# Five of eight row pairs as seven block products from the third gate-up group, and the first pair's lower parts on GpSimd

## The chip, the cores and the metric

One core of a Trainium2 chip runs the whole layer as one program. The metric is the device time of one execution in microseconds (us), median of several runs. TensorE (PE in the profile) multiplies matrices, VectorE (DVE), ScalarE (ACT) and GpSimd (POOL) work element by element, SyncE (SP) and GpSimd issue the DMA transfers.

## The reference

A layer on 256 tokens of width 2048: a feed-forward network (FFN1), a mixer with a recurrence and windowed attention, and a second FFN. Each FFN is, with weights of 2048 x 11264 and 5632 x 2048 in float32,

```python
def swiglu(x, w_gate_up, w_down):
    gate, up = jnp.split(x @ w_gate_up, 2, axis=-1)
    return (jax.nn.silu(gate) * up) @ w_down

ff = swiglu(rms_norm(x, pre_norm_ffn1[layer]), w_ffn1_gate_up[layer], w_ffn1_down[layer])
x = x + 0.5 * rms_norm(ff, post_norm_ffn1[layer])
```

## The kernel before

**Parts.** Each float32 operand is split into an upper part h, a rounded copy made by ScalarE, and a lower part l = x - h, made by VectorE (`split_act`, L175 to L177). A product of two blocks is three matmuls: h h, l h, h l (`three`). Weights come as tiles `raw` of 128 x 2048 float32 (1 MB), each holding four blocks of 128 x 512: two row blocks by the gate and the up columns. `split_half` makes h and l of 1024 columns at once.

**Groups and pairs.** The gate-up stage of an FFN (`Gated`, `ffn`) runs over 11 groups of 512 gate and 512 up columns, numbered 0 to 10. A group goes over the 2048 rows in eight pairs, 0 to 7, of two row blocks of 128, and accumulates a 2 x 2 grid of PSUM banks c (two token halves by gate and up).

**Plain and seven.** A pair is multiplied plainly, as eight block products (24 matmuls), or in Winograd's form, as seven (21 matmuls). The four pairs of `MIXED_IN`, 2, 4, 5 and 6, are sevens from group 2. A seven needs sums of the left blocks, made once (`sums_of`, four blocks S1 to S4), and sums of the right blocks for each tile: an accumulating DMA issued by GpSimd adds two blocks of the weights onto the tile (`add_second`), two VectorE adds (L985, L986) do the rest. Its order on VectorE is: lower part of the first block, 512 wide and some pairs ahead (`prepare`); then, in `splits`, the lower part of the second half of the tile ("lower"), the two adds, the lower part of the first half ("upper"), that of the changed second half ("last").

**The fold.** Four of the seven products go to banks p of their own. At the end of a group `boundary` folds these into c by eight VectorE adds (L1194 to L1204), each with one input in PSUM, between the products of pairs 6 and 7, and TensorE adds pair 7 to each bank behind its add. Then the parts of the next group's pair 0 are made, then the silu of the gate on ScalarE (L1110) and the product with the up half on VectorE (L1115), four transposes each, and ht, the parts of the down projection's input, with its own sums for some groups (L394 to L398, `MIXED_EARLY`: those of the first eight groups).

**What sets the order.** Everything from group 1 on is under `tc.manual_schedule()`, so each engine takes its instructions in the order in which the code makes them:

```python
for g in range(1, NG):
    first_pairs(g, waiting)
    for u in range(2, last - 1):
        pair_ahead(g, u)
    ...
    boundary(g, gated.splits(g + 1, 0) if g < NG - 1 else splits(0))
```

`pair_ahead(g, u)` makes the parts of pair u + 1 and lets TensorE multiply pair u. The pools hold five h, five l and five `raw` tiles. `plan` and `PREPARED` set the order in which tiles are loaded; a tile's next load is issued on SP once its last part is made (`load_next`). In FFN1's group 1 pair 6 is plain, and its sums are made in that group behind pair 6's parts (`sums_in`).

Of the kernel before, what the change touches and what calls it, by code (L numbers as in the profile page):

```python
# [11 lines left out]
F32 = mybir.dt.float32  # L12
F32R = mybir.dt.float32r
# [4 lines left out]
ALU = mybir.AluOpType  # L18
AX = mybir.AxisListType

P = 128
D = 2048
T = 256
# [25 lines left out]
def hymba_layer_kernel(  # L49
# [19 lines left out]
    nc = tc.nc  # L69
# [4 lines left out]
    hip = ctx.enter_context(tc.tile_pool(name="hip", bufs=5))  # L74
    lop = ctx.enter_context(tc.tile_pool(name="lop", bufs=5))
# [5 lines left out]
    def nm(s):  # L81
        uid[0] += 1
        return f"{s}_{uid[0]}"
# [81 lines left out]
            ls.append(l)  # L165
        return hs, ls

    def split_half(raw, i, hp=hip, lp=lop):
        part = raw[:, i * 1024 : (i + 1) * 1024]
        h = hp.tile([P, 1024], F32R, tag="h", name=nm("h"))  # L170
        l = lp.tile([P, 1024], F32R, tag="l", name=nm("l"))
        split_act(h, l, part)
        return h, l

    def split_act(hi, lo, src):  # L175
        nc.scalar.copy(hi, src)  # L176
        nc.vector.tensor_tensor(lo, src, hi.bitcast(F32), ALU.subtract)  # L177


    def rsqrt_of(ssq, scale, eps):  # L180
# [211 lines left out]
    def sums_of(u, w):  # L392

        nc.vector.tensor_tensor(  # L394
            w[:, S3::2, :], u[:, 0, :].rearrange("p (m t) -> p m t", m=2), u[:, :, P:T], ALU.subtract
        )
        nc.vector.tensor_tensor(w[:, S2, :], w[:, S1, :], u[:, 0, 0:P], ALU.subtract)
        nc.vector.tensor_tensor(w[:, S4, :], u[:, 1, 0:P], w[:, S2, :], ALU.add)  # L398
        return w

    class Blocks:
# [67 lines left out]
        def products(self, u, first, lower, upper, last, order=range(7)):  # L469

            if not self.p:
                self.p = [pa(), pa(), pb(), pb()]
            a, w = self.tiles[u], self.left_sums(u)

            def lhs(k, m):
                return [a[:, k, i, m * P : (m + 1) * P] for i in range(2)]

            def summed(j):
                return [w[:, j, i, :] for i in range(2)]

            def rhs(two, n):
                return [x[:, n * 512 : (n + 1) * 512] for x in two]

            seven = (
                (("p", 0), lhs(0, 0), first),
                (("c", 0, 0), lhs(1, 0), rhs(lower, 1)),
                (("c", 0, 1), summed(S4), rhs(lower, 0)),
                (("p", 1), summed(S1), rhs(upper, 0)),
                (("p", 3), summed(S3), rhs(upper, 1)),
                (("p", 2), summed(S2), rhs(last, 0)),  # L490
                (("c", 1, 0), lhs(1, 1), rhs(last, 1)),
            )
            for i in order:
                at, left, right = seven[i]
                self.three(at, *left, *right)
# [399 lines left out]
    NG = DFF // 512  # L895
# [2 lines left out]

    MIXED_IN = (2, 4, 5, 6)
    PREPARED = {2: -0.5, 4: 0.5, 5: 1.5, 6: 3.5}  # L900
    AWAY = 8
    MIXED = range(0, 20, 2)
    MIXED_EARLY = MIXED[:8]
# [11 lines left out]
    class Gated(Blocks):  # L915
# [23 lines left out]
        def plan(self, opened=False):  # L939

            some = MIXED_IN[1:3] if opened else MIXED_IN[:3]
            self.here = {g: MIXED_IN if g > 1 else some for g in range(1, NG)}
            wanted = []
            for g in range(1, NG):
                for u in range(KT // 2):
                    before = PREPARED[u] if u in self.here[g] else u
                    wanted.append((g * KT // 2 + before, g, u))
            self.wanted = [at[1:] for at in sorted(wanted)]
            self.raws, self.firsts, self.split_of = {}, {}, {}
            self.lasting = []  # L950
            pools = ((rawp, 3), (self.room, 2))
            for pool, n in pools[:: -1 if opened else 1]:
                for _ in range(n):
                    raw = pool.tile([P, 2048], F32, tag="raw", name=nm("raw"), bufs=n)
                    if pool is rawp:
                        self.lasting.append(raw)
                    self.load_next(raw)
# [10 lines left out]
        def prepare(self, g, u):  # L968

            if u not in self.here.get(g, ()):  # L970
                return
            raw = self.raws[g, u]
            h, l = (self.room.tile([P, 512], F32R, tag=t, name=nm(t), bufs=3) for t in ("h1", "l1"))
            split_act(h, l, raw[:, 0:512])
            add_second(raw, self.source(u, g))
            self.firsts[g, u] = h, l

        def splits(self, g, u):

            raw = self.raws[g, u]  # L980
            got = self.split_of[g, u] = []
            if (g, u) in self.firsts:
                b11, b12, b22, b21 = (raw[:, i * 512 : (i + 1) * 512] for i in range(4))
                got.append(split_half(raw, 1))
                nc.vector.tensor_tensor(b22, b11, b22, ALU.add)  # L985
                nc.vector.tensor_tensor(b21, b22, b21, ALU.add)  # L986
                yield
                got.append(split_half(raw, 0))
                yield
                got.append(split_half(raw, 1))  # L990
                self.load_next(raw)
            else:
                got.append(split_half(raw, 0))
                yield
                got.append(split_half(raw, 1))
                self.load_next(raw)
            yield

# [43 lines left out]
    def ffn(gated, w_dn, post_gain, again, gain=None, lead=None, opening=None):  # L1042

        with ExitStack() as st:
# [3 lines left out]
            early = early_cm.__enter__()  # L1048
# [5 lines left out]
            def room_for(tag):  # L1054
                return work.tile([P, 512], F32, tag=tag, name=nm(tag))
# [7 lines left out]
            def sums_again(u):  # L1063

                ht = hts[u].bitcast(F32)
                w = far["pool"].tile([P, 4, P], F32, tag=f"su{u}", name=nm("su"), bufs=1)
                nc.vector.tensor_tensor(
                    w.rearrange("p (k m) t -> p k (m t)", k=2), ht[:, :, 0, :], ht[:, :, 1, :], ALU.add
                )
                a11, a21, a12, a22 = (w[:, i, :] for i in range(4))  # L1070
                nc.vector.tensor_tensor(a22, a21, a22, ALU.subtract)
                nc.vector.tensor_tensor(a21, a11, a21, ALU.subtract)
                nc.vector.tensor_tensor(a11, a22, a11, ALU.subtract)
                nc.vector.tensor_tensor(a12, a12, a11, ALU.add)
                return w

            def even(u):

# [14 lines left out]
            def sums_in(u):  # L1093
                split_act(*sums_begin(u))
# [113 lines left out]
            def first_pairs(g, waiting):  # L1208

                gated.group(g)  # L1210
                some(waiting, 1)
                gated.prepare(g, MIXED_IN[1])
                some(waiting, 1)
                ahead = gated.splits(g, 1)
                some(ahead, 2)
                gated.prepare(g, MIXED_IN[2])
                for one in gated.take(g, 0):
                    one()
                some(waiting, 1)
                ahead = gated.splits(g, 2)  # L1220
                some(ahead, 2)
                some(waiting, 1)
                next(ahead, None)
                for one in gated.take(g, 1):
                    one()

            def pair_ahead(g, u):

                ahead = gated.splits(g, u + 1)
                next(ahead)  # L1230
                if u + 1 == MIXED_IN[1]:
                    gated.prepare(g, MIXED_IN[3])
                next(ahead)
                for one in gated.take(g, u):
                    one()
                for _ in ahead:
                    pass
                if g == 1 and u in sums_at:
                    sums_in(sums_at[u])
                if u == 5 and 1 < g <= AWAY // 2 + 1:  # L1240
                    put_away(2 * g - 4)
                    put_away(2 * g - 3)
# [86 lines left out]
            with tc.manual_schedule():  # L1329
# [3 lines left out]
# [4 lines that stand above are left out]
                    some(gated.splits(g, last), 2)  # L1337
                    if g < NG - 1:
                        gated.prepare(g + 1, MIXED_IN[0])
                    for one in gated.take(g, last - 1):  # L1340
                        one()
                    boundary(g, gated.splits(g + 1, 0) if g < NG - 1 else splits(0))
                    waiting = units(gated.c, rest)
                    some(waiting, 2)
                room_cm.__exit__(None, None, None)
# [290 lines left out]
    with ExitStack() as s2:  # L1636
# [665 lines left out]
        g = gates(1)  # L2302
# [167 lines left out]
```

## Time and profile before

| | |
|---|---|
| median of 3 runs | 1808.65 us (1808.06 to 1808.78) |
| profiled execution | 1808.42 us, its span 1806.6 us |
| TensorE matmuls busy | 1794.5 us, 99% |
| VectorE busy | 1654.2 us, 92% |
| ScalarE busy | 1132.8 us, 63% |
| GpSimd busy | 130.1 us, 7% |

Busy time is the union of an engine's records. Matmuls overlap, so a busy TensorE need not be at its peak. The granted clock of TensorE is 0.999 of 2.4 GHz in the mean. The folds of FFN1's groups 1 and 2 start at 87.27 and 129.10 us, those of groups 6 and 7 at 296.32 and 338.14.

### The profile page before, as it was taken

Reading aid. Unit: us, or ns where it says so; the run is one execution under the profiler, and the core shown is the slowest. Engines: PE = TensorE matmul, PEld = TensorE weight load, DVE = VectorE, ACT = ScalarE, POOL = GpSimd, SP = SyncE. Lnnn points to the kernel's source line nnn. Section 1 sums busy time; section 2 is a strip of 40 time slices with the busy share of each in tenths; the row PEclk is TensorE's granted clock in tenths of the full one; section 3 lists DMA queues with packets and bytes.
Section 4 is the critical chain, followed back from the end, with each engine's and each line's share of the span. In section 5 each row is a group of like instructions: output and inputs, shape, how many; then the busy total and the mean of one; then the engine's idle time right before and its main releaser. Section 6 shows DMA issues by size and latency. Waiting matters only on the chain.

```text
span 1806.6 us, 23864 instructions
## 1 busy us (share of the span) xinstructions
PE 1794.5 (99%) x8368; PEld 1491.4 (83%) x8368; DVE 1654.2 (92%) x2150; ACT 1132.8 (63%) x1487; POOL 130.1 (7%) x158
## 2 busy tenths in 40 slices
PE   9999999999999999999999999999999999999998
PEld 7888888888888888888899888888888888888886
DVE  6999999999999999888888888899999999999997
ACT  7566666655656666566767666556666566566663
POOL 0000000000000101000000000000000000000010
PEclk9999999999999999999999999999999999999999
DMA  9789998888799997954555767889989888699994
GB/s 371 231 256 279 273 277 256 257 259 218 253 324 305 307 285 248 290 158 165 177 169 169 255 198 273 246 238 280 277 270 275 251 248 253 196 318 340 280 315 161
DMA packets 128024, 460.63 MB, mean 255 GB/s; under 512 B 14353, under 2 KB 17169, under 8 KB 126369
## 3 DMA queue, kind: packets, MB, share of 16 engines
q1 hardware_dynamic: 109152, 391.18, 60.9%
q0 software_dynamic: 18608, 67.68, 21.3%
q8 instruction: 65, 1.06, 0.2%
q14 instruction: 55, 0.44, 0.1%
q10 hardware_dynamic: 144, 0.26, 0.0%
HBM read 444.38 MB, written 14.68 MB: 254 GB/s over the span
## 4 chain that ended last, share of the span: by engine, by line
PE 93%; DVE 3%; DMA 2%; ACT 1%; issue 1%; SPq 0%; POOL 0%; DVEq 0%; ACTq 0%; POOLq 0%
PE pa L443 43%; PE pb L443 37%; PE pa L315 6%; PE pa L320 3%; DVE l L177 1%; DMA raw<-in_w_ffn_gate_up_dram 1%; PE pb L1766 1%; DMA X<-in_x_dram 1%; PE pb L1135 1%; PE pa L1135 1%; PE pa L369 0%; PE pa L368 0%; PE pa L367 0%; PE pb L2065 0%; ACT xt L227 0%
## 5 line engine op out<-in xcount | busy, mean ns | idle before, releaser
L176 ACT CAST h<-raw 128x1024 fp32r<-128x1024 f32 (+1 forms) x849 | 831.8, 1009 | 429.9 <-PE pb L443 140.4
L177 DVE TENSOR_TENSOR l<-raw,h 128x1024 fp32r<-128x1024 f32 (+1 forms) x849 | 960.8, 1166 | 75.4 <-ACT h L176 57.0
L443 PE MATMUL pa<-h,xt 128*128 128x512 f32 x1198 | 420.5, 392 | 0.2 <-DVE xt L232 0.2
L443 PE MATMUL pb<-h,xt 128*128 128x512 f32 x1044 | 373.1, 391 | 0.4 <-DVE pb L1197 0.4
L443 PEld LDWEIGHTS pa<-h,xt 128*128 128x128 f32 x1198 | 225.0, 188 | 48.5 <-DVE xt L232 0.6
L443 PEld LDWEIGHTS pb<-h,xt 128*128 128x128 f32 x1044 | 195.9, 188 | 46.9 <-DVE pb L1204 3.8
L443 PE MATMUL pa<-l,xt 128*128 128x512 f32 x599 | 233.6, 390 | 0.0
L443 PE MATMUL pb<-l,xt 128*128 128x512 f32 x522 | 203.3, 390 | 0.0
L443 PE MATMUL pb<-h,ht 128*128 128x512 f32 x428 | 151.2, 389 | 0.0
L443 PE MATMUL pa<-h,ht 128*128 128x512 f32 x428 | 151.1, 389 | 0.0
L443 PEld LDWEIGHTS pa<-l,xt 128*128 128x128 f32 x599 | 112.6, 188 | 22.6 <-DVE l L177 0.7
L148 POOL DMA_DIRECT2D raw<-in_w_ffn_gate_up_dram x77 | 67.3, 874 | 766.2 <-DVE l L177 736.3
L443 PE MATMUL pa<-h,xs 128*128 128x512 f32 x328 | 117.2, 389 | 0.0
L443 PE MATMUL pb<-h,xs 128*128 128x512 f32 x328 | 114.3, 389 | 0.0
L443 PEld LDWEIGHTS pb<-l,xt 128*128 128x128 f32 x522 | 98.0, 188 | 18.9
L315 PE MATMUL pa<-xt,h 128*128 128x512 f32 x448 | 109.9, 393 | 0.0
L315 PEld LDWEIGHTS pa<-xt,h 128*128 128x128 f32 x448 | 81.5, 188 | 15.3
L443 PEld LDWEIGHTS pb<-h,ht 128*128 128x128 f32 x428 | 80.4, 188 | 16.6
L443 PEld LDWEIGHTS pa<-h,ht 128*128 128x128 f32 x428 | 80.3, 188 | 16.6
L443 PE MATMUL pa<-l,ht 128*128 128x512 f32 x214 | 83.3, 389 | 0.0
L443 PE MATMUL pb<-l,ht 128*128 128x512 f32 x214 | 83.3, 389 | 0.0
L443 PEld LDWEIGHTS pa<-h,xs 128*128 128x128 f32 x328 | 61.6, 188 | 12.7
(340 smaller groups left out, 2531.7 us busy)
## 6 DMA issues: line engine op xcount, KB each, us to landing
raw<-in_w_ffn_gate_up_dram SPq DMA_DIRECT2D x350, 512.0 KB, 6.3
raw<-in_w_ffn_down_dram SPq DMA_DIRECT2D x176, 512.0 KB, 8.3
raw<-in_w_mix_in_dram SPq DMA_DIRECT2D x94, 512.0 KB, 4.8
raw<-in_w_ffn_gate_up_dram POOLq DMA_DIRECT2D x77, 512.0 KB, 8.3
raw<-in_w_ffn_down_dram POOLq DMA_DIRECT2D x42, 512.0 KB, 8.7
ht<-away SPq DMA_DIRECT2D x24, 512.0 KB, 10.5
raw<-in_w_mix_out_dram SPq DMA_DIRECT2D x24, 512.0 KB, 5.5
away<-ht SPq DMA_DIRECT2D x16, 512.0 KB, 7.4
```

The costliest lines, as they stand in the source:

```text
L148: nc.gpsimd.dma_start(raw[:, 0:1024], src[:, 512:1536], accum_op=ALU.add)
L176: nc.scalar.copy(hi, src)
L177: nc.vector.tensor_tensor(lo, src, hi.bitcast(F32), ALU.subtract)
L315: nc.tensor.matmul(slot[f], weights(hs, kk, f), xcol(xt, k), start=(k == 0), stop=(k == KT - 1))
L320: nc.tensor.matmul(slot[f][:, 0:T], weights(ls, kk, f), xcol(xt, kh * 8 + kk, 0), start=False, stop=False,)
L443: nc.tensor.matmul(self.bank(at), lhs, rhs, start=(n == 1), stop=n in (ends, self.of[at]), skip_group_check=n > ends,)
L1135: nc.tensor.transpose(bank[:, o : o + P], zs[m][:, k * P : (k + 1) * P], ident)
L1766: nc.tensor.matmul(dst, left[a], right[b], start=first and i == 0, stop=last and i == 2)
```

## The change

From group 3 (`FIVE_FROM`) pair 3 is a seven too, so that the sevens are 2 to 6. The sums of pair 3's left blocks are made in group 2 (`sums_apart`) and put into places of the x tiles that sevens don't read. The first block of pair 5 gets a buffer of its own (`spare`), and the loading order follows `PREPARED_FIVE`. The lower parts of pair 0 of groups 2 to 10 are subtracted on GpSimd (`by=nc.gpsimd`).

```diff
-    def split_half(raw, i, hp=hip, lp=lop):
+    def split_half(raw, i, hp=hip, lp=lop, by=nc.vector):
...
-    def split_act(hi, lo, src):
+    def split_act(hi, lo, src, by=nc.vector):
         nc.scalar.copy(hi, src)
-        nc.vector.tensor_tensor(lo, src, hi.bitcast(F32), ALU.subtract)
+        by.tensor_tensor(lo, src, hi.bitcast(F32), ALU.subtract)
...
     MIXED_IN = (2, 4, 5, 6)
     PREPARED = {2: -0.5, 4: 0.5, 5: 1.5, 6: 3.5}
+    ADDED = 3
+    FIVE = (2, 3, 4, 5, 6)
+    PREPARED_FIVE = {2: -0.5, 3: 0.5, 4: 1.5, 5: 2.5, 6: 3.5}
+    FIVE_FROM = 3
...
-            self.here = {g: MIXED_IN if g > 1 else some for g in range(1, NG)}
+            self.here = {
+                g: FIVE if g >= FIVE_FROM else MIXED_IN if g > 1 else some for g in range(1, NG)
+            }
...
+            if g >= FIVE_FROM and u == FIVE[3]:
+                h, l = self.spare(g)
...
-                got.append(split_half(raw, 0))
+                got.append(split_half(raw, 0, by=by))
                 yield
-                got.append(split_half(raw, 1))
+                got.append(split_half(raw, 1, by=by))
                 self.load_next(raw)
...
+            def sums_apart(u):
+                x = gated.tiles[u].bitcast(F32)
+                whole = room_for("z").rearrange("p (k t) -> p k t", k=2)
+                nc.vector.tensor_tensor(whole, x[:, :, 0, :], x[:, :, 1, :], ALU.add)
+                ws = sums_of(whole, room_for("s").rearrange("p (j t) -> p j t", j=4))
+                gated.sums[u] = [
+                    [gated.tiles[v][:, 0, i, P:T] for i in range(2)] for v in MIXED_IN
+                ]
+                for j, (hi, lo) in enumerate(gated.sums[u]):
+                    split_act(hi, lo, ws[:, j, :])
...
+                if u == 2 and g >= FIVE_FROM:
+                    gated.prepare(g, FIVE[3])
...
+                if u == 5 and g == FIVE_FROM - 1:
+                    sums_apart(ADDED)
...
-                    boundary(g, gated.splits(g + 1, 0) if g < NG - 1 else splits(0))
+                    boundary(g, gated.splits(g + 1, 0, nc.gpsimd) if g < NG - 1 else splits(0))
```

Over the program TensorE has 48 matmuls of 512 columns fewer, VectorE 44 instructions more, ScalarE 40, and GpSimd 52: 36 subtractions of 128 x 1024 and 16 DMA issues.

On VectorE, behind the fold that closes group 5 of FFN1, there stood before (`l_...` of 1024 columns from `raw_486` are pair 0's lower parts, the 512-wide one is the first block of pair 4, `raw_489` is pair 1):

```order
L1204 TENSOR_TENSOR pb_1982<-pb_1982,s_2285 128x512
L177 TENSOR_TENSOR l_2320<-raw_486,h_2319 128x1024
L177 TENSOR_TENSOR l_2324<-raw_486,h_2323 128x1024
L1115 SCALAR_TENSOR_TENSOR z_2329<-pa_1980,scales,z_2329 128x512
L177 TENSOR_TENSOR l_419_2339<-raw_492,h_418_2338 128x512
L1115 SCALAR_TENSOR_TENSOR s_2331<-pb_1982,scales,s_2331 128x512
L177 TENSOR_TENSOR l_2345<-raw_489,h_2344 128x1024
```

and there stands now, at the same place (the 512-wide one is the first block of pair 3):

```order
L1237 TENSOR_TENSOR pb_2009<-pb_2009,s_2318 128x512
L1148 SCALAR_TENSOR_TENSOR z_2362<-pa_2007,scales,z_2362 128x512
L177 TENSOR_TENSOR l_428_2372<-raw_486,h_427_2371 128x512
L1148 SCALAR_TENSOR_TENSOR s_2364<-pb_2009,scales,s_2364 128x512
L177 TENSOR_TENSOR l_2378<-raw_489,h_2377 128x1024
```

Pair 0's two subtractions are gone from between the fold and the gate products; they are on GpSimd. On VectorE in the same group pair 3 was, between the last part of pair 2 (`raw_483`) and the first of pair 4 (`raw_492`):

```order
L177 TENSOR_TENSOR l_2415<-raw_483,h_2414 128x1024
L177 TENSOR_TENSOR l_2445<-raw_486,h_2444 128x1024
L177 TENSOR_TENSOR l_2449<-raw_486,h_2448 128x1024
L177 TENSOR_TENSOR l_2480<-raw_492,h_2479 128x1024
L985 TENSOR_TENSOR raw_492<-raw_492 128x512
```

and is now (`h_240_1402` is the spare buffer, for the first block of pair 5):

```order
L177 TENSOR_TENSOR l_2448<-raw_483,h_2447 128x1024
L177 TENSOR_TENSOR l_2478<-raw_486,h_2477 128x1024
L997 TENSOR_TENSOR raw_486<-raw_486 128x512
L998 TENSOR_TENSOR raw_486<-raw_486 128x512
L177 TENSOR_TENSOR h_240_1402<-raw_495,h_240_1402 128x512
L177 TENSOR_TENSOR l_2487<-raw_486,h_2486 128x1024
L177 TENSOR_TENSOR l_2516<-raw_486,h_2515 128x1024
L177 TENSOR_TENSOR l_2522<-raw_492,h_2521 128x1024
```

Two instructions of pair 3 became five, and the first block of pair 5 moved in among them. On VectorE in FFN1's group 2 the new sums stand between the last part of pair 6 (`raw_489`) and pair 7's parts (`raw_483`), ahead of the next group's first block and the fold:

```order
L177 TENSOR_TENSOR l_1177<-raw_489,h_1176 128x1024
L1102 TENSOR_TENSOR z_1182<-xt_124 128x512
L394 TENSOR_TENSOR s_1184<-z_1182 128x2x128
L397 TENSOR_TENSOR s_1184<-s_1184,z_1182 128x128
L398 TENSOR_TENSOR s_1184<-z_1182,s_1184 128x128
L177 TENSOR_TENSOR xt_124<-s_1184,xt_124 128x128
L177 TENSOR_TENSOR xt_125<-s_1184,xt_125 128x128 x3
L177 TENSOR_TENSOR l_1201<-raw_483,h_1200 128x1024
```

Eight instructions are new there; ScalarE has four casts of 128 x 128 at the same place.

## Rows read from the trace of the kernel before

**Rows 1.** Stretches: us, busy us (instructions) by engine, granted clock, DMA share, GB/s.

```profile
129.10:170.90 41.80, 41.80 (x190) 34.46 (x189) 39.82 (x48) 26.18 (x31) 3.49 (x4) 1.00 0.93 277
379.90:421.70 41.80, 41.80 (x190) 34.48 (x189) 38.98 (x45) 25.45 (x30) 3.51 (x4) 1.00 0.88 253
492.83:600.00 107.17, 107.17 (x473) 88.54 (x473) 103.92 (x128) 70.02 (x88) 10.53 (x12) 1.00 0.96 301
```

**Rows 2.** Chain that ended last, in order of time: start, us, what.

```profile
357.29 2.72 PE pa L443 x12
```

**Rows 3.** Waits of TensorE's weight loads: us in total, times, longest.

```profile
PEld pb L443 <- DVE pb L1204: 3.8, 18, 0.2
```

**Rows 4.** Timeline of VectorE from one fold on: start, us, instruction [idle before].

```profile
296.32 0.69 DVE L1194 TENSOR_TENSOR pa<-pa,z 128x512 f32<-128x512 f32 x1
...
301.90 2.35 DVE L177 TENSOR_TENSOR l<-raw,h 128x1024 fp32r<-128x1024 f32 x2
304.16 0.74 DVE L1115 SCALAR_TENSOR_TENSOR z<-pa,scales,z 128x512 f32<-128x512 f32 x1
304.82 0.68 DVE L177 TENSOR_TENSOR l<-raw,h 128x512 fp32r<-128x512 f32 x1
305.42 0.75 DVE L1115 SCALAR_TENSOR_TENSOR s<-pb,scales,s 128x512 f32<-128x512 f32 x1
306.09 4.09 DVE L177 TENSOR_TENSOR l<-raw,h 128x1024 fp32r<-128x1024 f32 x4
...
312.68 0.69 DVE L177 TENSOR_TENSOR ht<-z,ht 128x512 fp32r<-128x512 f32 x1
...
314.88 3.48 DVE L177 TENSOR_TENSOR l<-raw,h 128x1024 fp32r<-128x1024 f32 x3
318.64 1.22 DVE L177 TENSOR_TENSOR l<-raw,h 128x1024 fp32r<-128x1024 f32 x1 [0.28 <-ACT h L176]
319.90 0.69 DVE L985 TENSOR_TENSOR raw<-raw 128x512 f32<-128x512 f32 x1
...
321.23 4.12 DVE L177 TENSOR_TENSOR l<-raw,h 128x512 fp32r<-128x512 f32 x4
```

**Rows 5.** Timeline of VectorE ahead of that fold, pairs 5 and 6.

```profile
287.07 2.59 DVE L177 TENSOR_TENSOR l<-raw,h 128x1024 fp32r<-128x1024 f32 x2 [0.81 <-ACT h L176]
...
291.03 5.38 DVE L177 TENSOR_TENSOR l<-raw,h 128x1024 fp32r<-128x1024 f32 x5
```

**Rows 6.** Timeline of ScalarE around that fold.

```profile
287.34 1.06 ACT L176 CAST h<-raw 128x1024 fp32r<-128x1024 f32 x1 [0.31 <-PE pb L443]
...
302.67 4.93 ACT L176 CAST h<-raw 128x512 fp32r<-128x512 f32 x6
```

**Rows 7.** Timeline of TensorE in that fold: the last matmul of bank c[0][1].

```profile
301.90 0.40 PE L443 MATMUL pa<-h,xt 128*128 128x512 f32 x1
```

**Rows 8.** Timeline of VectorE in FFN1's group 1, sums of pair 6.

```profile
80.96 0.68 DVE L1084 TENSOR_TENSOR z<-xt 128x512 f32<-128x512 f32 x1
...
84.39 2.96 DVE L177 TENSOR_TENSOR l<-raw,h 128x1024 fp32r<-128x1024 f32 x3 [0.26 <-ACT h L176]
```

**Rows 9.** Timeline of TensorE in the fold behind them.

```profile
90.14 0.50 PE L443 MATMUL pb<-h,xt 128*128 128x512 f32 x1 [0.40 <-DVE pb L1197]
```

**Rows 10.** Timelines of GpSimd (a fold; the end) and of VectorE (the end).

```profile
296.76 0.88 POOL L148 DMA_DIRECT2D raw<-in_w_ffn_gate_up_dram  x1 [15.42 <-DVE l L177]
...
1800.65 1.26 POOL L769 TENSOR_TENSOR X<-X,y 128x512 f32<-128x512 f32 x1 [0.83 <-ACT y L768]
...
1800.53 1.53 DVE L784 SCALAR_TENSOR_TENSOR X<-pb,r,X 128x512 f32<-128x512 f32 x3
```

**Rows 11.** Accumulating DMA issues: all of gate-up; single ones. KB, us to landing.

```profile
raw<-in_w_ffn_gate_up_dram POOLq DMA_DIRECT2D x77, 512.0 KB, 8.3
...
raw<-in_w_ffn_gate_up_dram POOLq DMA_DIRECT2D x1, 512.0 KB, 6.8
raw<-in_w_ffn_gate_up_dram POOLq DMA_DIRECT2D x1, 512.0 KB, 9.9
```

More of the change, by code (lines that the diff above doesn't have):

```diff
@@ L171, in split_half @@
         l = lp.tile([P, 1024], F32R, tag="l", name=nm("l"))
-        split_act(h, l, part)
+        split_act(h, l, part, by)
         return h, l
-    def split_act(hi, lo, src):
+    def split_act(hi, lo, src, by=nc.vector):
         nc.scalar.copy(hi, src)
-        nc.vector.tensor_tensor(lo, src, hi.bitcast(F32), ALU.subtract)
+        by.tensor_tensor(lo, src, hi.bitcast(F32), ALU.subtract)
     def rsqrt_of(ssq, scale, eps):
@@ L478, in summed @@
             def summed(j):
-                return [w[:, j, i, :] for i in range(2)]
+                return w[j] if isinstance(w, list) else [w[:, j, i, :] for i in range(2)]
             def rhs(two, n):
@@ L945, in plan @@
                 for u in range(KT // 2):
-                    before = PREPARED[u] if u in self.here[g] else u
+                    at = PREPARED_FIVE if g >= FIVE_FROM else PREPARED
+                    before = at[u] if u in self.here[g] else u
                     wanted.append((g * KT // 2 + before, g, u))
@@ L972, in prepare @@
             raw = self.raws[g, u]
-            h, l = (self.room.tile([P, 512], F32R, tag=t, name=nm(t), bufs=3) for t in ("h1", "l1"))
+            if g >= FIVE_FROM and u == FIVE[3]:
+                h, l = self.spare(g)
+            else:
+                h, l = (
+                    self.room.tile([P, 512], F32R, tag=t, name=nm(t), bufs=3) for t in ("h1", "l1")
+                )
             split_act(h, l, raw[:, 0:512])
@@ L976, in prepare, with splits @@
             self.firsts[g, u] = h, l
-        def splits(self, g, u):
+        def splits(self, g, u, by=nc.vector):
             raw = self.raws[g, u]
@@ L1075, in sums_again, with spare @@
                 return w
+            spared = {}
+            def spare(g):
+                pool = early if g < AWAY - 1 else late
+                if pool not in spared:
+                    spared[pool] = pool.tile([P, 2, 512], F32R, tag="ht", name=nm("h1"))
+                return [spared[pool][:, i, :] for i in range(2)]
+            gated.spare = spare
+            def sums_apart(u):
[8 more added lines that the diff above has]
+                    split_act(hi, lo, ws[:, j, :])
             def even(u):
@@ L1211, in first_pairs @@
                 some(waiting, 1)
-                gated.prepare(g, MIXED_IN[1])
+                sevens = FIVE if g >= FIVE_FROM else MIXED_IN
+                gated.prepare(g, sevens[1])
                 some(waiting, 1)
@@ L1215, in first_pairs @@
                 some(ahead, 2)
-                gated.prepare(g, MIXED_IN[2])
+                gated.prepare(g, sevens[2])
                 for one in gated.take(g, 0):
```

## The prediction

> **What bounds the kernel now.** I read three views in turn: the stretches by group, the waits of TensorE's weight loads, and VectorE's timeline through one gate-up group. In a middle group of FFN1 TensorE is busy for the whole 41.80 us and VectorE for 39.82, or 38.98 in a group without the small sums for the down projection; the granted clock is 1.00 [rows 1]. TensorE starts a matmul of 512 columns every 2.72/12 = 0.2267 us [rows 2]. So TensorE is the bound, but only just: at 18 of the 20 group boundaries it already waits up to 0.2 us for VectorE's last fold add, L1204 [rows 3]. The reader should see there that the fold at a boundary has no slack: what reaches it later is lost.
>
> VectorE's 39.82 us is not its whole need, since records overlap and dependent ones leave gaps, so I count from start to start. I call the start of L1194 in a fold T. From [rows 4]: the fold's eight adds take 301.90 - 296.32 = 5.58; pair 0's two 1024-wide lower parts 304.16 - 301.90 = 2.26, or 1.13 each; the two gate products 0.66 and 0.67, with a 512-wide lower part of 0.60 between; ht and sums 314.88 - 312.68 = 2.20. In a seven the first lower part with its following add takes 319.90 - 318.64 = 1.26 and the two adds 321.23 - 319.90 = 1.33. A seven therefore needs 0.60 + 1.26 + 1.33 + 2 x 1.13 = 5.45, a plain pair 2.26. A group before: 4 x 5.45 + 4 x 2.26 + 5.58 + 1.33 + 2.20 = 39.95 of 41.82; the other 1.87 is waiting. Most of that waiting is for ScalarE's upper part (0.28 in [rows 4], 0.81 in [rows 5], more in starts that leave no idle record), and ScalarE in turn waits for TensorE to release one of five buffers [rows 6]. So VectorE cannot run further ahead than those buffers let it. It meets the fold just in time in every group.
>
> **What TensorE saves.** A pair as seven products takes 21 matmuls for 24. Eight groups in each of two FFNs: 16 x 3 x 0.2267 = 10.9 us, 0.68 per group. A group would be 41.82 - 0.68 = 41.14.
>
> **What VectorE gets.** From group 3 pair 3 costs 5.45 for 2.26, and pair 0's 2.26 leaves for GpSimd: 5 x 5.45 + 2 x 2.26 + 9.11 = 40.88. That would fit below 41.14 if nothing waited; but four waits remain or appear, and each follows from the order of the instructions.
> - In pairs 5 and 6 the last part needs ScalarE's cast, which starts after the second add. [Rows 5] show five subtractions at 291.03 in 5.38, where 4 x 1.13 + 0.68 = 5.20; I take 0.14 for each: 0.28.
> - Pair 0's two subtractions stood between the fold and the first gate product, and covered the time in which TensorE finishes the bank that the product reads. That bank's last matmul ends at 301.90 + 0.40 = 302.30, T + 5.98 [rows 7]; with 0.07 for the signal the product starts at T + 6.05, not T + 5.58: 0.47 lost.
> - The next, 512-wide, subtraction needs a cast that ScalarE starts at 302.67, behind the two gate activations [rows 6]; at about 0.6 for it, a little over half of the 1.06 that 1024 takes there, that is T + 6.95, when VectorE is free at 6.05 + 0.66 = 6.71: 0.24.
> - 0.13 for two casts that come a little late (ht, pair 4's lower part): my estimate.
>
> Sum 40.88 + 1.12 = 42.00: VectorE, not TensorE, sets the group, and it is 0.18 longer than before. Bounds: waits of nothing give 41.14 (TensorE's), all of the former 1.87 give 42.75. Added up in order, such a cycle reaches T + 8.2 with the gate products, 10.5 with pair 1, 11.1 with the first block of pair 4, 18.2 with pair 2, ht and sums, 23.6 with pair 3 (first block of pair 5 at 21.4), 29.1 with pair 4 (first block of 6 at 26.8), 34.1 with pair 5, 39.1 with pair 6, and the next fold at 42.0. TensorE starts pair 2 at T + 19.0 and one seven every 4.76 after it, so the parts are ready for it, and of the buffers none holds VectorE: only the fold is late. Groups 3 to 8 carry the small sums, 9 and 10 do not: their 2.20 - 2 x 0.60 = 1.0 leaves 41.0, below 41.14, and the whole 0.68 is won. Per FFN: 6 x 0.18 - 2 x 0.68 = -0.3.
>
> **The new sums for pair 3.** They are made once per FFN, in group 2, behind the last part of pair 6 and ahead of pair 7's parts, with four casts on ScalarE ahead of pair 7's first cast. Behind them stand pair 7, the next group's first block and the fold. The trace has nearly this in group 1: the same three sums and one 512-wide split, at the same place. They take 84.39 - 80.96 = 3.43 until pair 7's subtraction starts [rows 8], and TensorE then stood idle 0.40 in the fold [rows 9]. It lost so little because in group 1 pair 6 is plain, which costs VectorE 5.45 - 2.26 = 3.2 less and TensorE 0.68 more. In group 2 pair 6 is a seven, and VectorE comes to this place pinned by the buffers of [rows 5, 6], so what it saved early in the group on pair 0 is no lead. The cost is 3.43 at least; four narrow casts for one wide make it at most 3 x 0.6 more, 5.2. A quarter of the width is nearer to the lower end: 3.8. Hidden wholly, as most of it was in group 1, it would be 0.
>
> **GpSimd's part.** Its 512-wide add of two SBUF tensors took 1.265 beside VectorE's L784, which reads PSUM, and those three kept their usual 1.53 together [rows 10]. 1024 wide I take twice that at most, 2.53. It starts behind the DMA issue that ends at 296.76 + 0.88 = 297.64, T + 1.3 [rows 10]; two end by T + 6.4. The fold's adds, each with one input in PSUM, fill that time, and VectorE's next subtraction stands at T + 6.95; TensorE reads pair 0 from T + 7.2 (six matmuls behind the bank of [rows 7]). So I cost it at nothing. If it ended later, each further us would hold up pair 0.
>
> **DMAs.** 16 more accumulating loads of 512 KB. A group then moves 277 x 41.8 + 524 KB, near 12.1 MB in 42.0 us: 288 GB/s. The down stage had 301 with TensorE never idle [rows 1]. In time it is closer: behind their issue, the loads of pairs 5 and 6 have about 8.6 and 8.2 us before the adds that read them (first block done at T + 21.4 and 26.8, issue 0.4 later, adds at 30.4 and 35.4). The median landing is 8.3, one of pair 6, the last of its group, took 6.8, a slow one 9.9 [rows 11]. I take no wait, since these two stand in the quieter part of the group, as that of 6.8 did; 9.9 - 8.2 = 1.7 is the bound.
>
> **The sum.** Per FFN 3.8 - 0.3 = 3.5; twice, 7.0. The profiled execution took 1808.42 (span 1806.6 and 1.8 around it), 0.23 under the median of 1808.65. 1808.42 + 7.0 = 1815.4. Its own range: sums at 3.4 to 5.2 and the cycle 0.2 either way, so 1812 to 1821.
>
> **Rivals.**
> - Faster: VectorE is not the bound. If its waits come to 0.26 or less per group for my 1.12 and the sums are hidden as in group 1, the 10.9 is kept: 1797.5. For it speaks that idle time of 1.87 stands there today; against it that the ledger leaves 0.26. Chance 0.12.
> - The sums are hidden, the rest as forecast: 1808.42 - 0.6 = 1807.8. Against it: group 2's seven at pair 6. 0.08.
> - The sums cost, but groups stay TensorE's: 1808.42 + 7.6 - 10.9 = 1805.1. 0.07.
> - The accumulating loads come late, 0.5 to 1.7 in each of 12 to 16 groups, say 1 in 14: 1815.4 + 14 = 1829. The landing times allow it. 0.13.
> - GpSimd blocks VectorE. If a subtraction of VectorE could not start or run while GpSimd's is under way, 36 x 2.53 = 91 would be added at worst, 1906; it decides once GpSimd ends later than T + 6.95. Against it: [rows 10], and 0.5 us of room. 0.03. The Trainium skill (SBUF — State Buffer, "SBUF: two separate sides") states such a lock: GpSimd and a VectorE instruction with two SBUF inputs exclude each other for a whole instruction. By that rule the fold, with one input in PSUM, runs beside GpSimd, and the trace agrees as far as L784 shows; no row has the other pairing.
>
> **The numbers.** The forecast has 0.57. What this kernel's measurement can tell is about 0.2%, 3.6 us: slower is the forecast, the late loads and the lock, 0.73; same the two middle rivals, 0.15; faster 0.12. A range of 1804.5 to 1825 holds the forecast, the middle rivals and half of the late loads, some 0.8.
>
> **What would show it.** Folds 42.0 apart in groups 3 to 8 and 41.1 in 9 and 10; TensorE waiting some 0.9 per fold for L1230 and L1234; 45.6 between the folds of groups 1 and 2, TensorE idle about 3.8 at the second; GpSimd's two subtractions inside the fold at 2.3 to 2.5 each; VectorE waiting before the first gate product. I am wrong if folds lie 41.1 apart throughout, or if VectorE stands waiting for the accumulating loads before L997, or if fold adds beside GpSimd's subtractions run longer than 0.7.

## The result and the profile after

The changed kernel takes 1826.36 us (median of 4 runs, 1825.73 to 1827.27) against 1808.57 (4 runs, 1808.06 to 1808.78): 1.0100 times as long, 95% interval 1.0087 to 1.0112. The forecast was 1815.4, with a range to 1825.0. The sign was right, the size was not: slower by 17.8 us, not 7. The profiled execution took 1825.73 us, its span 1824.0 (before 1806.6), at a granted clock of 0.999.

From the page of the changed kernel: busy time by engine, and the chain that ended last, by engine.

```profile
PE 1794.1 (98%) x8320; PEld 1480.8 (81%) x8320; DVE 1668.3 (91%) x2194; ACT 1149.3 (63%) x1527; POOL 228.4 (13%) x210
PE 72%; DVE 14%; DMA 7%; issue 4%; ACT 2%; SPq 0%; DVEq 0%; POOL 0%; ACTq 0%
```

TensorE has 48 matmuls fewer, yet its union of records is as long as before (1794.5): the shares of busy time say nothing of the loss. The chain does: before, 93% of it was TensorE; now 21% of it is VectorE and DMA.

In the lines after, the fold is L1227 to L1237 (before L1194 to L1204), the gate products L1148, the two adds of a seven L997 and L998. From the starts of L1227 in VectorE's timeline come the distances between one fold and the next, in us; "group 2" ends with the fold that closes group 2.

| | 2 | 3 | 4 | 5 | 6 | 7 | 8 | 9 | 10 |
|---|---|---|---|---|---|---|---|---|---|
| FFN1 before | 41.83 | 41.80 | 41.81 | 41.80 | 41.81 | 41.82 | 41.81 | 41.79 | 41.20 |
| FFN1 after | 45.22 | 42.46 | 42.03 | 43.16 | 42.46 | 42.67 | 43.11 | 42.09 | 41.49 |
| FFN2 before | 41.83 | 41.80 | 41.82 | 41.79 | 41.81 | 42.06 | 41.79 | 41.81 | 41.19 |
| FFN2 after | 45.21 | 42.96 | 42.94 | 43.14 | 42.05 | 42.91 | 42.65 | 42.08 | 41.46 |

Summed over both FFNs, after less before: group 2 +6.8; groups 3 to 8 +10.6, of which 12 x 0.22 = 2.6 is the undisturbed distance of 42.03 and 8.0 lies above it; groups 9 and 10 +1.1. That is 18.5; the rest of the program gave 1.1 back, which makes the span's 17.4.

The waits of the changed kernel, us in total, times, longest (before, TensorE waited 3.8 us for the last fold add [rows 3]):

```profile
PEld pa L443 <- DVE pa L1227: 16.9, 16, 2.7
PEld pb L443 <- DVE pb L1230: 16.4, 20, 0.9
DVE raw L997 <- DMA raw<-in_w_ffn_gate_up_dram: 7.5, 10, 1.1
DVE z L1148 <- PE pa L443: 6.4, 18, 0.4
```

TensorE waits at every fold for VectorE, as forecast, though in 16 of the 20 at the first add already and not only from L1230 on. New, and in the forecast only as a rival and a sign of being wrong, is that VectorE stands ten times at the first add of a seven. VectorE's timeline through FFN1's group 5 shows where (start, us, instruction [idle before]; it answers to [rows 4, 5]):

```profile
217.18 0.69 DVE L1227 TENSOR_TENSOR pa<-pa,z 128x512 f32<-128x512 f32 x1
...
223.20 0.75 DVE L1148 SCALAR_TENSOR_TENSOR z<-pa,scales,z 128x512 f32<-128x512 f32 x1 [0.35 <-PE pa L443]
224.17 0.69 DVE L177 TENSOR_TENSOR l<-raw,h 128x512 fp32r<-128x512 f32 x1 [0.22 <-ACT h L176]
...
253.70 0.69 DVE L997 TENSOR_TENSOR raw<-raw 128x512 f32<-128x512 f32 x1 [0.68 <-DMA raw<-in_w_ffn_gate_up_dram]
254.43 0.69 DVE L998 TENSOR_TENSOR raw<-raw 128x512 f32<-128x512 f32 x1
255.04 5.38 DVE L177 TENSOR_TENSOR l<-raw,h 128x1024 fp32r<-128x1024 f32 x5
260.34 0.69 DVE L1227 TENSOR_TENSOR pa<-pa,z 128x512 f32<-128x512 f32 x1
```

With T = 217.18 the gate product starts at T + 6.02 and the block at T + 6.99 (forecast 6.05 and 6.95). At T + 36.5 the adds of pair 6 wait 0.68 for their accumulating load, and behind them only the last two parts of pair 6, pair 7 and one block are left before the fold, so that the fold is late by what they wait. All ten waits stand at this place, pair 6's first add, each in another group from 3 to 8. In eight of these groups the distance lies above 42.03 by that wait, within 0.03; in the other two (FFN1's group 5 and FFN2's group 8) 0.4 more lies elsewhere. GpSimd's timeline of the same group:

```profile
217.62 0.86 POOL L148 DMA_DIRECT2D raw<-in_w_ffn_gate_up_dram  x1 [14.30 <-DVE l L177]
218.19 5.08 POOL L177 TENSOR_TENSOR l<-raw,h 128x1024 fp32r<-128x1024 f32 x2
...
245.10 0.86 POOL L148 DMA_DIRECT2D raw<-in_w_ffn_gate_up_dram  x1 [4.73 <-DVE l L177]
```

The two subtractions run from T + 1.01 to T + 6.09, beside the fold and the wait behind it. The load for pair 6 is issued at 245.10 and would have been read at 253.70 - 0.68 = 253.02, 7.9 us on; the median landing of these loads is now 8.6 us (8.3 before [rows 11]).

In groups 9 and 10 no add waits for a load, and still the fold is later than before. VectorE's and ScalarE's timelines in FFN1's group 9:

```profile
388.58 0.69 DVE L1227 TENSOR_TENSOR pa<-pa,z 128x512 f32<-128x512 f32 x1
...
406.19 1.23 DVE L177 TENSOR_TENSOR l<-raw,h 128x1024 fp32r<-128x1024 f32 x1 [0.35 <-ACT h L176]
...
410.95 2.59 DVE L177 TENSOR_TENSOR l<-raw,h 128x1024 fp32r<-128x1024 f32 x2 [0.34 <-ACT h L176]
...
430.67 0.69 DVE L1227 TENSOR_TENSOR pa<-pa,z 128x512 f32<-128x512 f32 x1
```

```profile
409.87 1.05 ACT L176 CAST h<-raw 128x1024 fp32r<-128x1024 f32 x1 [0.98 <-PE pa L443]
```

At T + 22.4 VectorE, at pair 3's last part, waits for a cast, which waits for TensorE to release a buffer. From there to the next fold it works without a pause: 430.67 - 410.95 = 19.7 us. 22.4 + 19.7 is the 42.09 of the table, whatever spare time VectorE had earlier in the group.

### The profile page after: what moved, and what is told of

Its sections match the earlier page's. It is cut to its first block, busy times and chain, and to the rows that moved or that the text cites. A ratio compares the mean times of both kernels' runs of the same rounds, so it can differ in the third digit from the quotient of the medians.

```text
span 1824.0 us, 23998 instructions
## 1 busy us (share of the span) xinstructions
PE 1794.1 (98%) x8320; PEld 1480.8 (81%) x8320; DVE 1668.3 (91%) x2194; ACT 1149.3 (63%) x1527; POOL 228.4 (13%) x210
## 4 chain that ended last, share of the span: by engine, by line
PE 72%; DVE 14%; DMA 7%; issue 4%; ACT 2%; SPq 0%; DVEq 0%; POOL 0%; ACTq 0%
PE pa L443 31%; PE pb L443 28%; DVE l L177 7%; PE pa L315 6%; DMA raw<-in_w_ffn_gate_up_dram 6%; PE pa L320 3%; ACT h L176 2%; DVE raw L997 1%; DVE raw L998 1%; PE pa L369 1%; PE pa L368 1%; PE pa L367 1%; DVE pb L1230 1%; DVE z L1229 1%; PE pb L1804 1%
## 5 line engine op out<-in xcount | busy, mean ns | idle before, releaser
L176 ACT CAST h<-raw 128x1024 fp32r<-128x1024 f32 (+1 forms) x881 | 850.1, 1002 | 399.1 <-DVE raw L1346 85.6
L177 DVE TENSOR_TENSOR l<-raw,h 128x1024 fp32r<-128x1024 f32 (+1 forms) x829 | 936.1, 1166 | 64.9 <-ACT h L176 47.3
L443 PE MATMUL pb<-h,xt 128*128 128x512 f32 x1012 | 363.4, 394 | 7.9 <-DVE pb L1230 7.8
L443 PEld LDWEIGHTS pb<-h,xt 128*128 128x128 f32 x1012 | 190.1, 188 | 59.4 <-DVE pb L1230 16.4
L443 PE MATMUL pa<-l,xt 128*128 128x512 f32 x583 | 228.0, 391 | 0.0
L443 PE MATMUL pb<-l,xt 128*128 128x512 f32 x506 | 197.5, 390 | 0.0
L148 POOL DMA_DIRECT2D raw<-in_w_ffn_gate_up_dram x93 | 81.0, 871 | 687.3 <-DVE l L177 498.8
L177 POOL TENSOR_TENSOR l<-raw,h 128x1024 fp32r<-128x1024 f32 x36 | 91.3, 2722 | 0.0
L148 POOL DMA_DIRECT2D raw<-in_w_ffn_down_dram x42 | 36.4, 866 | 378.6 <-DVE la L177 328.6
```

The source lines that it names most:

```text
L148: nc.gpsimd.dma_start(raw[:, 0:1024], src[:, 512:1536], accum_op=ALU.add)
L177: by.tensor_tensor(lo, src, hi.bitcast(F32), ALU.subtract)
L443: nc.tensor.matmul(self.bank(at), lhs, rhs, start=(n == 1), stop=n in (ends, self.of[at]), skip_group_check=n > ends,)
```

## The experiments

Each is an edit of the changed kernel; folds are counted as in the table. "Before" ran beside them at 1808.85 (the new sums left out, and both repairs), at 1808.75 (GpSimd's part alone, the sevens alone, the sums earlier, the loads earlier) and at 1808.91 (the other four).

### GpSimd's part alone

No group has a fifth seven; GpSimd keeps pair 0.

```diff
-    FIVE_FROM = 3
+    FIVE_FROM = 99
```

> Four sevens as before, no new sums, pair 0's lower parts of groups 2 to 10 on GpSimd. Theory (GpSimd runs beside the fold at no cost, VectorE has 1.87 us of waiting per group that takes up the new wait of 0.35 to 0.47 before the first gate product): folds 41.8 us apart, 1808 to 1809.5. Rival (the new waits behind the fold, 0.57 per group, or a block of VectorE by GpSimd, are lost in full): 18 x 0.57 = 10 us or more, 1819 and up.

1808.33 us (10 runs), ratio 0.9998 (0.9989 to 1.0008). Folds 41.79 to 41.82 apart, 41.2 in group 10. The wait for the gate product is there (18 times, 6.9 us) and costs nothing, since VectorE waits later in the group anyway. So beside four sevens GpSimd's part is free, and what the change loses comes with the fifth.

### The sevens alone

Pair 0's lower parts go back to VectorE.

```diff
-  boundary(g, gated.splits(g + 1, 0, nc.gpsimd) if g < NG - 1 else splits(0))
+  boundary(g, gated.splits(g + 1, 0) if g < NG - 1 else splits(0))
```

> The changed kernel with pair 0's lower parts left on VectorE. Theory (VectorE sets the group): each group from 3 on gets 2.26 us of work more and loses the waits of 0.35 and 0.22 behind the fold, 1.7 x 16 = 27 us, 1850 to 1856. Rival (GpSimd's subtractions hold VectorE up about as much as they take from it): 1820 to 1832.

1843.77 us, ratio 1.0194 (1.0179 to 1.021): below the band expected, and far above the rival's. The undisturbed distance in groups 3 to 8 is 43.50, 1.47 more than with GpSimd. The ledger gives 2.26 less the 0.47 and 0.24 that pair 0 covers again, 1.55. Waits of 0.2 to 1.3 for loads stand in eight of those groups, and no wait for casts is left. Groups 3 to 8 add 14.6 us to the changed kernel's, groups 9 and 10 2.5, of which 0.8 is a wait for a load in FFN2's group 9: in those the two waits for casts (0.35 and 0.34 in the changed kernel's group 9) are gone, so that a part of the added work fills them.

### The new sums left out

Pair 3 takes the sums of pair 2, so the output is not the layer's.

```diff
                 if u == 5 and g == FIVE_FROM - 1:
-                    sums_apart(ADDED)
+                    gated.sums[ADDED] = gated.sums[MIXED_IN[0]]
```

> The changed kernel without the new sums: pair 3 is multiplied with the sums of pair 2, so its output is not the layer's, and the eight VectorE instructions and four ScalarE casts of group 2 are left out. If the sums cost what the distance of the folds of groups 1 and 2 says, the fold that closes group 2 comes 41.8 us behind the one before (45.2 with the sums), everything behind stays as it is in the changed kernel, and the time is 1826.4 - 2 x 3.4 = 1819.6. Rival: the delay in group 2 gave later groups a lead in their loads, which is lost without it; then the waits for the accumulating loads of pair 6 grow and the time stays above 1822.

1820.28 us, ratio 1.0063 (1.0048 to 1.0078): 6.1 less than the changed kernel. Group 2 takes 41.82 and 41.81. Groups 9 and 10 stay within 0.02; groups 3 to 8, with nine waits for loads, take 1.1 more together, single ones from 0.9 less to 1.1 more. The sums cost 3.4 per FFN at their place.

### The sums earlier in group 2

```diff
-                if u == 5 and g == FIVE_FROM - 1:
+                if u == 2 and g == FIVE_FROM - 1:
                     sums_apart(ADDED)
```

> The changed kernel with pair 3's sums made in group 2 behind pair 3's parts, not behind pair 6's. Theory (the sums cost 3.4 us per FFN because nothing but the fold follows them; earlier, VectorE's waiting for buffers takes them up): folds of groups 1 and 2 some 41.8 to 42.3 apart instead of 45.2, 1819 to 1820.5. Rival (VectorE has no time for them anywhere in group 2): 1825 to 1827.

1821.67 us, ratio 1.0072 (1.0057 to 1.0087). Group 2 takes 43.17 and 43.16 where 41.8 to 42.3 was expected: of 3.4 only 2.0 came back. The run without the sums shows what can take them up. VectorE's timeline in its group 2 (FFN1, T = 87.36):

```profile
107.64 1.23 DVE L177 TENSOR_TENSOR l<-raw,h 128x1024 fp32r<-128x1024 f32 x1 [0.83 <-ACT h L176]
109.68 1.22 DVE L177 TENSOR_TENSOR l<-raw,h 128x1024 fp32r<-128x1024 f32 x1 [0.81 <-ACT h L176]
...
119.92 2.59 DVE L177 TENSOR_TENSOR l<-raw,h 128x1024 fp32r<-128x1024 f32 x2 [0.81 <-ACT h L176]
```

At T + 20.3, 22.3 and 32.6 VectorE waits for casts, which wait for TensorE to release a buffer. Work ahead of such a wait can fill it. Behind the sums' place in the changed kernel stands none of the three, behind the new place two. The run with both repairs (below) has the sums behind ht, ahead of all three, and group 2 takes 42.29 and 42.27. The same eight instructions cost 3.4, 1.35 or 0.47 by how many of these waits stand behind them. (Behind ht the load of pair 6 came late besides in three of eight cases, by 0.46 to 0.96, in FFN2 of other runs below.)

### The loads of pairs 5 and 6 earlier

Their first blocks, behind which the loads are issued, are made earlier: that of pair 5 behind ht, that of pair 6 one pair sooner.

```diff
                 some(waiting, 1)
+                if g >= FIVE_FROM:
+                    gated.prepare(g, FIVE[3])
                 next(ahead, None)
...
-                if u == 2 and g >= FIVE_FROM:
-                    gated.prepare(g, FIVE[3])
-                if u + 1 == MIXED_IN[1]:
+                if u + 1 == (3 if g >= FIVE_FROM else MIXED_IN[1]):
                     gated.prepare(g, MIXED_IN[3])
```

> The changed kernel with the first blocks of pairs 5 and 6, and so their accumulating loads, some 4 and 5 us earlier from group 3. Theory (in groups 3 to 8 the folds are 42.4 to 43.2 apart for 42.0 because these loads have 8 us and take longer): VectorE's waits for DMA at the first add go from 7.5 us to under 1, folds near 42.1, 1817 to 1820. Rival (16 more loads fill the DMA engines): the waits stay, 1824 to 1828.

1822.74 us, ratio 1.0078 (1.0063 to 1.0093): 3.6 less, half of what was expected. No add waits for a load any more, yet groups 3 to 8 give back only 2.9 of the 8 that they had too much; 1.7 more come from groups 9 and 10, and the rest of the program lost 1.4 in the profiled execution. Of groups 3 to 8 five lie at 42.17 to 42.23 (0.14 over 42.03, since one cast in pair 5 lost the subtraction that covered it); seven have 42.3 to 42.9, with waits between T + 4 and T + 12, most of them for casts. Ordinary loads play a part in these: by the order of its casts, ScalarE's waits for them in groups 3 to 8 come to 16.8 us in this run and to at most 4.6 in the changed kernel (its other 29.5 us there are for accumulating loads). So one wait was in part exchanged for another.

The more telling rows are in group 9. VectorE's timeline there:

```profile
388.26 0.69 DVE L1227 TENSOR_TENSOR pa<-pa,z 128x512 f32<-128x512 f32 x1
...
409.73 3.50 DVE L177 TENSOR_TENSOR l<-raw,h 128x1024 fp32r<-128x1024 f32 x3 [0.26 <-ACT h L176]
```

Its work per group is the same, but the block of pair 6 (0.60) now stands ahead of the last wait, which is at pair 3's upper part, one instruction earlier than in the changed kernel. From pair 3's last part to the fold VectorE now works for 19.0 us (an estimate, with 1.13 for the upper part) instead of 19.7. Groups 9 and 10 fall to 41.64 and 41.05 (42.09 and 41.49 in the changed kernel). What sets their length is when the buffer comes and the work behind it, not the sum of the work.

### Five sevens in groups 9 and 10 alone

Groups without small sums and without late loads; the new sums are made in group 8, behind ht.

```diff
-    FIVE_FROM = 3
+    FIVE_FROM = 9
...
+                if g == FIVE_FROM - 1:
+                    sums_apart(ADDED)
...
-                if u == 5 and g == FIVE_FROM - 1:
-                    sums_apart(ADDED)
```

> Five sevens in groups 9 and 10 alone, the sums in group 8 behind ht; all else as before, with GpSimd's part. Theory (from the last buffer that TensorE releases VectorE has 19.7 us of work to the fold while TensorE needs less, so the fold is late though the group's sum of work is small): folds 8 to 9 and 9 to 10 at 42.1 and 41.5 apart, for 41.8 and 41.2, 1809 to 1811. Rival (what counts is the sum of VectorE's work, 41.0): 41.14 and 40.5, 1805 to 1807.

1811.33 us (10 runs), ratio 1.0014 (1.0004 to 1.0023). The folds that close groups 9 and 10 come after 42.06 and 41.48 in FFN1 (42.75, with a wait of 0.46 for TensorE within the fold before and one of 0.34 for a cast at T + 33.7, and 41.49 in FFN2). Group 8, with the sums, takes 42.25 and 43.19, the latter with a late load of 0.96. Of the 41.1 that my ledger gives for them nothing is to be seen, though in FFN1 nothing but their own work and the release is left to delay them.

### A block ahead of the gate products

The sums behind ht, the early loads, and the first block of pair 3 between the fold and the gate products, to fill the 0.47 in which VectorE waits there.

```diff
-                gated.prepare(g, sevens[1])
+                if g < FIVE_FROM:
+                    gated.prepare(g, sevens[1])
...
                     boundary(g, gated.splits(g + 1, 0, nc.gpsimd) if g < NG - 1 else splits(0))
+                    if FIVE_FROM <= g + 1 < NG:
+                        gated.prepare(g + 1, FIVE[1])
```

> The changed kernel with the early loads of e3, pair 3's sums still earlier in group 2 (behind ht, ahead of pair 2's last part), and the first block of pair 3 cast and subtracted between the fold and the gate products, where VectorE waited 0.35 and 0.22. Theory (VectorE sets groups 3 to 8, so a wait filled there is won): least distance of folds in 3 to 8 from 42.17 in e3 to 41.6, group 2 at 41.8 to 42.2, 9 and 10 unchanged at 41.6 and 41.1; 1808 to 1812. Rival (the block, with two inputs in SBUF, meets GpSimd's second subtraction, which ends near T + 6.1, and waits for it): the block starts at T + 6.1 and not at T + 5.6, folds near 42.1, 1813 to 1817.

1817.57 us, ratio 1.0051 (1.0033 to 1.0069), just above the rival's band. Group 2 takes 42.27, and 43.19 in FFN2, where pair 6's load is 0.96 late. The undisturbed distance is 42.16 to 42.21, no shorter than with the early loads alone. Timelines of VectorE and of GpSimd at one fold of this run:

```profile
304.42 0.70 DVE L1237 TENSOR_TENSOR pb<-pb,s 128x512 f32<-128x512 f32 x1
305.03 1.07 DVE L177 TENSOR_TENSOR l<-raw,h 128x512 fp32r<-128x512 f32 x1
306.02 0.74 DVE L1148 SCALAR_TENSOR_TENSOR z<-pa,scales,z 128x512 f32<-128x512 f32 x1
```

```profile
300.45 5.08 POOL L177 TENSOR_TENSOR l<-raw,h 128x1024 fp32r<-128x1024 f32 x2
```

GpSimd ends at 305.53. The block starts at 305.03 and its record is 1.07 long, where this form takes 0.68: it ended 0.57 behind GpSimd, as if it had begun only then. In all 16 folds of this kind it ended 0.55 to 0.57 behind GpSimd, whenever it had begun. The fold adds before it, with an input in PSUM, keep their 0.68 to 0.70 beside GpSimd. The filled wait came back as a block.

### Pair 1's lower parts on GpSimd too

```diff
-                ahead = gated.splits(g, 1)
+                ahead = gated.splits(g, 1, nc.gpsimd if g >= FIVE_FROM else nc.vector)
```

> The changed kernel with pair 1's two lower parts on GpSimd as well from group 3, at a time when VectorE has instructions with two inputs in SBUF. Theory A (no block between the engines): VectorE gets 2.26 us of 42 back, groups 3 to 8 fall to 41.1 to 41.7 apart, 1812 to 1818 with the sums' 6.8 still there. Theory B (GpSimd and such an instruction of VectorE exclude each other): VectorE's 1.13 us subtractions behind the gate products take up to 2.5 us longer, groups grow by 1 to 3 us, 1835 to 1870.

1868.83 us, ratio 1.0333 (1.0317 to 1.035). VectorE has 2.26 us less to do per group, and groups 3 to 8 take 45.0 to 46.4. VectorE's timeline, one instruction of it alone, and GpSimd's beside it:

```profile
279.96 3.98 DVE L177 TENSOR_TENSOR l<-raw,h 128x512 fp32r<-128x512 f32 x1 [1.94 <-ACT h L176]
```

```profile
278.34 5.05 POOL L177 TENSOR_TENSOR l<-raw,h 128x1024 fp32r<-128x1024 f32 x2
```

VectorE's block ends at 283.94, 0.55 behind GpSimd's second subtraction. All of that form, grouped by shape (times, busy us, mean ns), in this run and in the changed kernel:

```profile
L177 DVE TENSOR_TENSOR l<-raw,h 128x512 fp32r<-128x512 f32 x85 | 117.7, 1387 | 33.4 <-ACT h L176 33.4
```

```profile
L177 DVE TENSOR_TENSOR l<-raw,h 128x512 fp32r<-128x512 f32 x85 | 58.3, 688 | 8.5 <-ACT h L176 8.4
```

117.7 - 58.3 = 59.4 us over 16 groups, 3.7 in each. In the group shown the wait of 1.94 and the lengthening of 3.98 - 0.69 = 3.29, less the 2.26 of work, make 2.97; the group takes 45.42, of which 0.43 waits for a load: 44.99 - 42.03 = 2.96.

With the early loads and the sums behind ht added to this edit:

> e8 with the early loads and the earlier sums. Theory A: 1803 to 1809, groups 41.1 to 41.6. Theory B: 1828 to 1865.

1858.79 us, ratio 1.028 (1.0261 to 1.0298), groups 3 to 8 steady at 45.16 to 45.33: the block needs no late load to cost its 3 us.

### Both repairs, the block back in its place

The sums behind ht and the early loads of above.

> The changed kernel with the early issue of pairs 5 and 6 and with the new sums made behind ht of group 2, and the first block of pair 3 between the gate products as in the changed kernel. Theory (in the run with that block ahead of the gate products GpSimd's second subtraction held it up for 0.4 to 0.5 us, so that its move was worth nothing): folds of groups 3 to 8 at 42.2 as with that block ahead, group 2 at 42.3 to 43.2, and a time like that run's, 1816 to 1818.5. Rival (the block ahead of the gates did win, and something else lost it again): 1820 or more.

1815.74 us (5 runs, 1814.6 to 1817.94), ratio 1.0034 (1.002 to 1.0048). Group 2 takes 42.29 and 42.27; groups 3 to 8 lie between 42.17 and 43.9, most of the longer ones behind casts at T + 11 to 12; 9 and 10 take 41.65 and 41.06. Its interval overlaps that of the run with the block ahead, so the block's move was worth nothing that can be measured. It is the fastest version with five sevens from group 3 on, and it is still slower than the kernel before.

## Why the forecast missed

Two terms failed: the waits for accumulating loads, put at nothing, and groups 9 and 10, put at a gain.

| term of the sum, both FFNs, us | forecast | measured |
|---|---|---|
| new sums in group 2 | +7.6 | +6.8 |
| groups 3 to 8, undisturbed | +2.2 | +2.6 |
| groups 3 to 8, above that (waits for accumulating loads 7.5) | 0 | +8.0 |
| groups 9 and 10 | -2.7 | +1.1 |
| elsewhere | 0 | -1.1 |

- **VectorE's ledger for groups 3 to 8: right.** 42.00 forecast; undisturbed groups take 42.03 and 42.05. The waits behind the fold came as worked out, and the run without GpSimd confirms the price of pair 0 within 0.1.
- **The new sums: right, a little high.** 3.4 for 3.8; 3.38 from the first add (126.43) to pair 7's (129.81), as in group 1 [rows 8]. VectorE's and TensorE's timelines there:

```profile
126.43 0.69 DVE L1102 TENSOR_TENSOR z<-xt 128x512 f32<-128x512 f32 x1
...
129.81 2.96 DVE L177 TENSOR_TENSOR l<-raw,h 128x1024 fp32r<-128x1024 f32 x3 [0.65 <-ACT h L176]
```

```profile
133.44 0.50 PE L443 MATMUL pa<-h,xt 128*128 128x512 f32 x1 [2.32 <-DVE pa L1227]
...
135.56 0.50 PE L443 MATMUL pb<-h,xt 128*128 128x512 f32 x1 [0.46 <-DVE pb L1230]
```

  TensorE lost 2.32 and 0.46 in that fold, 2.8 where I expected 3.8.
- **"I take no wait" for the accumulating loads: the term that failed most.** It was sized at nothing with 1.7 as the bound; 10 of 12 groups waited, 7.5 us together. I allowed pair 6's load 8.2 us from issue to use and it has 7.9 in the group shown; I then set a median of 8.3 aside for one row of 6.8. A margin that lies on the median of a spread from 6.8 to 9.9 [rows 11] means a wait in about half of the groups; with 7.9 against a median of 8.6 it was more. The rival was named, at 0.13 and 14 us for the 7.5 measured. That these waits make the changed kernel's groups too long is shown by their size, group by group. That the loads' issue is behind them is shown too: issued earlier, no add waits. What is not shown is that the 8.0 can be won back: 1.7 of it went to the earlier blocks' new place (12 x 0.14) and 3.6 to waits early in the group, most of them for casts.
- **"9 and 10 do not: ... the whole 0.68 is won": failed.** The ledger compared a sum of work (41.0) with TensorE's 41.14. But VectorE cannot carry early spare time across the release of a buffer at T + 22.4. Behind it stand the last part of pair 3, pairs 4 to 7 and the next group's first block, 19.7 where 41.14 would have left 18.7; a seven takes VectorE 5.45 while TensorE needs 21 x 0.2267 = 4.76. I had both numbers, and wrote that "of the buffers none holds VectorE": it was held, by 0.34, with three sevens still ahead of it. Moving 0.60 of work ahead of the last wait shortened the group by 0.45, and the three places of the sums cost 3.4, 1.35 and 0.47. A sixth buffer was not tried.
- **GpSimd's part at nothing: right**, by itself and where it stands. I counted 0.5 us of room and there was 0.9: T + 6.1 against T + 7.0.
- **The lock, at 0.03: no cost in this change, and real.** Three runs put a subtraction of VectorE beside GpSimd's, and it stood until GpSimd had ended. The Trainium skill (SBUF — State Buffer, "SBUF: two separate sides") says that a GpSimd instruction and a VectorE instruction with two SBUF inputs exclude each other for a whole instruction; the traces agree, with 0.39 and 3.29 us of lengthening.

"Elsewhere" is not explained: from FFN1's last fold to FFN2's first the runs shown here differ by 2.5 us. Open too: why ordinary loads of gate-up weights come later than before, with a median of 6.7 us from issue to landing (6.3 before, 6.8 with the early loads). The stretches of FFN1's groups 3 and 9 (from fold to fold: us, busy us by engine, granted clock, DMA share, GB/s) answer to the first two of [rows 1]:

```profile
132.69:175.15 42.46, 41.25 (x184) 33.69 (x185) 40.62 (x50) 27.14 (x33) 9.08 (x7) 1.00 0.93 263
388.58:430.67 42.09, 40.88 (x182) 33.39 (x183) 39.92 (x48) 26.28 (x31) 9.14 (x7) 1.00 0.93 259
```

The DMA engines are no busier in group 3 (0.93 both times) and busier in group 9 (0.93 for 0.88), where no add waits for a load; no run here separates the 16 additional accumulating loads from the shorter time between a tile's last reader and its next use.

## What to carry to other kernels

Before crediting an engine with spare time, find the places in the cycle where it is held by a buffer, and count the work between the last of them and the deadline: an instruction cost its full length here behind that place, and less the more such waits still followed it (3.4, 1.35, 0.47). Hold the time from a transfer's issue to its use against the spread of landings, not against the friendliest row: a margin that was taken equal to the median was here a wait in ten of twelve groups. Work moved to GpSimd was free here beside VectorE instructions that read PSUM, and cost more than it saved beside those with two SBUF inputs.

## What the hardware showed that I had not expected

Where GpSimd had two subtractions in a row (5.05 us together), VectorE's subtraction, begun 1.62 us after the first one's start, did not get in between the two: it ended 0.55 us behind the second, after 3.98 us, and GpSimd's pair was no longer than elsewhere (5.08). A record of VectorE thus shows such a block as a long instruction and not as idle time; it is found by the mean of its form, 1387 ns for 688, and not among the waits.
